# Grouped attention: the weighted sums as plain fp32 products of 64 columns, one product per half of the array

## The chip, the cores and the metric

The kernel runs on one core of one Trainium2 chip. The metric is the device time of one execution in microseconds (us); a kernel's time is the median of several executions. TensorE multiplies matrices into PSUM; VectorE (DVE) and ScalarE (ACT) do the element-wise work, GpSimd (POOL) some filling of memory and some transfers, SyncE (SP) issues most transfers. A product on TensorE has a stationary operand that is loaded first (LDWEIGHTS, the engine row PEld) and a moving operand whose columns are streamed past it (MATMUL, the row PE).

## The reference

A decoder trunk of four layers on 256 tokens of width 2048, in float32. Layer 0 and layer 3 use latent attention, layer 1 sparse grouped attention (each query keeps the 64 keys that an indexer scores highest), layer 2 grouped attention in a window of 128 with a learned sink. Every layer adds four heads of attention to a memory, multiplies all heads by SiLU of a gate, and projects back:

```
for i in range(DEPTH):
    h = _rmsnorm(x, norm_in[i])
    self_out, mq, gate = mixer(h, ...)
    mem_out = _memory_attention(mq, mem_n @ w_mem_kv[i])
    y = concatenate([self_out, mem_out]) * silu(gate)
    x = x + y @ w_out[i]
```

The change touches one line of the two grouped mixers: the weighted sum of the values. There are 32 query heads of width 64 and 4 key/value heads, so that 8 query heads share one value matrix of 64 columns (layer 2 shown; layer 1 sums over the selected keys alone):

```
p = e / (sum(e) + exp(sink - m))
return einsum('bgjqk,bkgd->bqgjd', p, vb)      # j: the 8 heads of group g
```

## The kernel before, in words

All large products are split into parts: an fp32 operand is written as a high part in the format fp32r and a low remainder, also in fp32r, and a product becomes three fp32r products (high by high, high by low, low by high). ACT copies the high part (`copy_act`, L60) and DVE subtracts it to get the low one (L69); `split` does both. The weights `wr` come by DMA in pieces, are split into `wh` and `wl`, and go into `columns_by` (L277, L281) for the projections and into `rows_by` (L257, L258, L259) for the output projection.

Each layer runs over six parts, in the order 4, 0, 1, 2, 3, 5. Parts 4 and 5 are the two pairs of memory heads, parts 0 to 3 the four groups g of 8 heads. A part has a projection of queries (`acc_q`) and of the gate (`acc_g`), attention, and, one part later in the text of the program, its share of the output projection (`w_out`, accumulators `acc_wo`). Each `acc_wo` runs over four slices k of the part's result y: slices 0 and 1 come from the heads 0 to 3 of the group, slices 2 and 3 from the heads 4 to 7.

Within `Grouped.attend` the 8 heads go in the order 0, 2, 1, 3, 4, 6, 5, 7. For each head there are the scores `sp` (L949, L952), the softmax, the normalized weights transposed on TensorE into `ptp` (L516), and a copy of them into SBUF. Heads 0 and 2 share a tile (even), 1 and 3 another (odd), and so on: four heads make what is called a quartet below, and there are 16 quartets in the program (2 layers, 4 groups, 2 each). The weights are split into a high and a low tile of three blocks for each head: queries 0 to 127 by keys 0 to 127, queries 128 to 255 by keys 0 to 127, and queries 128 to 255 by keys 128 to 255. So the products over keys t=0 move 512 columns (2 blocks, 2 heads) and those over t=1 move 256.

The stationary operand is a window of 128 columns of `vz` (L801): the values of the groups, 64 columns each, with 64 columns of zeros between them. Beginning the window at the values or at the zeros before them puts the sum into the upper or the lower half of the 128 output rows and adds zero to the other half. So the even pair and the odd pair of a quartet accumulate into one PSUM tile `o` of 128 rows: rows 0 to 63 even, 64 to 127 odd. Each pair needs six products (two t, three combinations of parts), a quartet twelve (L978). Then DVE multiplies `o` by the gate (`yt`, L984) and splits it into y.

The order of instructions on each engine is not that of the text. A scheduler places them when the program is built, by simulating the engines' timelines; instructions that are marked `keep_in_program_order` keep their order among themselves. Softmax and weighted sums of one group are spread in this way over the projection of the next group and the output projection of the one before. Each engine then runs its own fixed queue in order.

Of the kernel before, what the change touches and what calls it, by code (L numbers as in the profile page):

```python
# [8 lines left out]
F32 = mybir.dt.float32  # L9
# [22 lines left out]
def kernel(ctx: ExitStack, tc: tile.TileContext, a: dict, out: bass.AP,  # L32
# [10 lines left out]
    def misc(name, dt=F32):  # L43
        return ps.tile([P, 512], dt, name=name, tag="mp", bufs=4)
# [8 lines left out]
    def f32(ap):  # L53
        return ap.bitcast(F32)
# [4 lines left out]
    def copy_act(o, i, scale=1.0):  # L59
        inst = nc.scalar.activation(o, i, AF.Copy, scale=scale)  # L60
        if pinned:
            tc.keep_in_program_order(inst)
# [4 lines left out]
    def split(hi, lo, src):  # L67
        copy_act(hi, src)
        nc.vector.tensor_sub(lo, src, f32(hi))  # L69
# [702 lines left out]
    class Grouped:  # L772
# [7 lines left out]
        def first(self):  # L780
            nm, w = self.nm, self.w
            acc = rows_by(nm.at, 16, w, 0, (self.kv0, 512), "kv")
            self.k = act.tile([P, 4, 2, S], F32R, name="kd", tag="big0")
            vs = act.tile([P, 4, S], F32, name="vs", tag="aux", bufs=AUX)
            self.v, self.sel = vs[:, :2, :], vs[:, 2:, :]
            for t in range(2):
                sc = nm.col("rstd", t)
                self.dup(lambda i0, i1: self.k.rearrange("p g v s -> p (g v) s")
                         [:, i0:i1, t * P:(t + 1) * P], acc[t][:, :S], sc, 4)
                copy_act(self.v[:, t, :], acc[t][:, S:], scale=sc)  # L790
            if self.sparse:
                steps.append(self.select())
            else:
                self.spaced_values()

        def spaced_values(self):


            self.vz = [act.tile([P, 2, 9 * 64], F32R, name="vz", tag=f"big{1 + z}") for z in range(2)]
            for z in range(2):  # L800
                nc.gpsimd.memset(f32(self.vz[z]), 0.0)  # L801
            for t in range(2):
                hi, lo = (self.vz[z][:, t, 64:].rearrange("p (g c) -> p g c", c=P)[:, :, :64] for z in range(2))
                split(hi, lo, self.v[:, t, :].rearrange("p (g c) -> p g c", c=64))

        def dup(self, dst, src, sc, n):

# [58 lines left out]
        def selection(self, iqT, ikd, iw, iw2):  # L866

            nc.gpsimd.memset(self.sel[:64, 0, :P], 0.0)
            for b in range(2):
                n = (b + 1) * P  # L870
                rows = slice(0, P) if b else slice(64, P)
                both = spare(0, "sco")
                sco = [both[:, z * S:(z + 1) * S] for z in range(2)]
                cur = 0
                for h in range((8, 16)[b]):
                    sp = misc("isp")
                    rl = wk.tile([P, S], F32, name="rl", tag="e", bufs=4)
                    if b == 0:

                        nc.tensor.matmul(sp[:, :S], iqT[0][:, 2 * h:2 * h + 2, :].rearrange("p h c -> p (h c)"),  # L880
                                         ikd[:, :, :P], start=True, stop=True)
                        lo = wk.tile([P, S], F32, name="isl", tag="z", bufs=3)
                        copy_act(lo[:, :P], sp[:, P:S])
                        nc.vector.tensor_add(lo[:, :P], lo[:, :P], sp[:, :P])
                        nc.scalar.activation(rl[:, :n], lo[:, :P], AF.Relu, scale=0.125)
                        c = iw2[:, h:h + 1]
                    else:
                        for v in range(2):
                            nc.tensor.matmul(sp[:, :S], iqT[1][:, h, :], ikd[:, v, :],
                                             start=v == 0, stop=v == 1)  # L890
                        nc.scalar.activation(rl[:, :n], sp[:, :n], AF.Relu, scale=0.125)
                        c = iw[:, 16 + h:17 + h]
                    if h == 0:
                        nc.vector.tensor_scalar(sco[0][:, :n], rl[:, :n], c, None, op0=OP.mult)
                    else:
                        nc.vector.scalar_tensor_tensor(sco[1 - cur][:, :n], rl[:, :n], c,
                                                       sco[cur][:, :n], op0=OP.mult, op1=OP.add)
                        cur = 1 - cur
                    yield True
                if b == 0:  # L900
                    even = wk.tile([P, S], F32, name="isl", tag="z", bufs=3)
                    nc.scalar.activation(even[64:, :n], sco[cur][:64, :n], AF.Copy)
                    nc.vector.tensor_add(sco[cur][64:, :n], sco[cur][64:, :n], even[64:, :n])
                nc.vector.tensor_add(sco[1 - cur][rows, :n], sco[cur][rows, :n], caus[rows, S - n:])
                cur = 1 - cur
                for it in range(8):
                    m8 = small("m8", 8)
                    nc.vector.max(m8[rows], sco[cur][rows, :n])
                    nc.vector.match_replace(sco[1 - cur][rows, :n], m8[rows], sco[cur][rows, :n], TAKEN)
                    cur = 1 - cur  # L910
                    yield True
                nc.vector.tensor_scalar(self.sel[rows, b, :n], sco[cur][rows, :n], -2e38, NEG,
                                        op0=OP.is_gt, op1=OP.mult)
            self.spaced_values()

        def heads_by_columns(self, dst, acc):

# [22 lines left out]
        def attend(self, g, q, bm, gT):  # L940
            while steps:
                other_work()
            y = act.tile([P, 2, 4, S], F32R, name="y", tag="y", bufs=2)
            for h in (0, 2, 1, 3, 4, 6, 5, 7):
                def score(b):
                    sp = misc("sp")
                    qb = q[h // 4][:, h % 4, b * P:(b + 1) * P]
                    if b == 0:
                        nc.tensor.matmul(sp[:, :S], qb, self.k[:, g, :, :P], start=True, stop=True)  # L949
                    else:  # L950
                        for v in range(2):
                            nc.tensor.matmul(sp[:, :S], qb, self.k[:, g, v, :],  # L952
                                             start=v == 0, stop=v == 1)
                    return sp

                def bias(b, n):
                    bh = bm[:, h, S - n:]
                    if not self.sparse:
                        return bh
                    bs = wk.tile([P, S], F32, name="bs", tag="e", bufs=4)  # L960
                    nc.vector.tensor_add(bs[:, :n], bh, self.sel[:, b, :n])
                    return bs[:, :n]
                nsk = None if self.sparse else nsink[:, g * 8 + h:g * 8 + h + 1]
                tp = masked_softmax(score, bias, None, nsk)

                half, odd = h // 2 % 2, h % 2
                if half == 0:
                    pHL = [wk.tile([P, 3, 2, P], F32R, name="pT2", tag="pT", bufs=PT) for z in range(2)]
                split(pHL[0][:, :, half, :], pHL[1][:, :, half, :],
                      tp[:, :3 * P].rearrange("p (i c) -> p i c", i=3))  # L970
                if half == 0:
                    continue
                if not odd:
                    o = misc("o")
                v0 = g * P + (0 if odd else 64)
                for t in range(2):
                    for n_, (z, p_) in enumerate(((0, 0), (0, 1), (1, 0))):
                        nc.tensor.matmul(o[:, t * S:], self.vz[z][:, t, v0:v0 + P],  # L978
                                         pHL[p_][:, 2 * t:2 + t].rearrange("p i h c -> p (i h c)"),
                                         start=odd == t == n_ == 0, stop=odd == t == 1 and n_ == 2)  # L980
                if odd:
                    j = (h // 4) * 2
                    yt = tmp("yt")
                    nc.vector.tensor_mul(yt.rearrange("p (j b c) -> p j b c", j=2, b=2),  # L984
                                         o.rearrange("p (b j c) -> p j b c", b=2, j=2),
                                         gT[:, j:j + 2, :].rearrange("p j (b c) -> p j b c", b=2))
                    split(y[:, 0, j:j + 2, :], y[:, 1, j:j + 2, :], yt.rearrange("p (a b) -> p a b", a=2))
            return y
# [243 lines left out]
```

## Time and profile before

| what | value |
|---|---|
| time, median of 3 runs | 2577.68 us (2577.62 to 2578.92) |
| span of the profiled execution, first to last instruction | 2576.5 us |
| PE busy, share of the span | 2560.7 us, 99% |
| PEld busy | 2212.3 us, 86% |
| DVE busy | 1928.4 us, 75% |
| ACT busy | 1616.6 us, 63% |
| granted TensorE clock, mean | 0.999 |
| the two grouped layers in the profile | about 980 to 1450 us and 1450 to 1930 us |

The profile shows one execution. Its own time as a run is not listed beside its span; the three runs lie 1.1 to 2.4 us above the span, the median 1.2. In the rows a time is us from the start of the span, and the number behind it the duration. Matmul records overlap at their ends: a record ends when its last results are modelled to be written, while the next has long begun to stream. What a product costs is therefore the distance from one record's end to the next one's, not its duration.

### The profile page before, as it was taken

How to read it: one execution, taken by the hardware profiler on the slowest of the kernel's cores; microseconds unless marked ns; L12 is line 12 of the kernel's file. 1: busy time of each engine (PE TensorE's matmuls, PEld its weight loads, DVE VectorE, ACT ScalarE, POOL GpSimd, SP SyncE). 2: the span in 40 equal slices, each digit the busy share in tenths (PEclk: the TensorE clock that was granted, in tenths of full speed). 3: DMA queues.
4: the chain of work that ended last, by engine and by line, in shares of the span. 5: the costliest groups of instructions: out<-in, count | busy, mean ns of one | idle time of the engine just before them, and what ended most of it. 6: DMA issues, size and time to landing. Idle time of an engine off the chain costs nothing.

```text
span 2576.5 us, 42094 instructions
## 1 busy us (share of the span) xinstructions
PE 2560.7 (99%) x14176; PEld 2212.3 (86%) x14176; DVE 1928.4 (75%) x4234; ACT 1616.6 (63%) x3460; POOL 82.5 (3%) x151
## 2 busy tenths in 40 slices
PE   9999999999999999999999999999999999999998
PEld 7888898888888889888888888888888888888887
DVE  6666667677777787978888777887878767777777
ACT  6556556556656566666666666676666655665665
POOL 1000000000000000000000000000000000000000
PEclk9999999999999999999999999999999999999999
DMA  9888777666677667565656575555554877676654
GB/s 301 256 258 265 241 213 235 186 169 193 196 200 218 203 214 237 169 203 183 204 167 188 168 227 172 172 176 190 185 161 145 241 201 196 195 197 183 210 175 180
DMA packets 477754, 520.04 MB, mean 202 GB/s; under 512 B 69425, under 2 KB 389825, under 8 KB 475873
## 3 DMA queue, kind: packets, MB, share of 16 engines
q1 hardware_dynamic: 460080, 449.71, 57.9%
q0 software_dynamic: 16736, 66.65, 8.1%
q8 instruction: 111, 1.82, 0.3%
q14 instruction: 107, 0.87, 0.1%
q10 hardware_dynamic: 720, 0.98, 0.1%
HBM read 494.10 MB, written 35.75 MB: 206 GB/s over the span
## 4 chain that ended last, share of the span: by engine, by line
PE 97%; DMA 1%; DVE 1%; ACT 0%; issue 0%; SPq 0%; ACTq 0%
PE acc_g L277 14%; PE acc_g L281 7%; PE acc_wo L257 6%; PE acc_wo L258 6%; PE acc_wo L259 6%; PE acc_mq L277 5%; PE acc_mk L277 5%; PE acc_q L277 5%; PE acc_cq L277 3%; PE acc_qn L277 3%; PE acc_mq L281 2%; PE acc_q L281 2%; PE acc_mk L281 2%; PE acc_mv L258 2%; PE acc_mv L257 2%; PE acc_mv L259 2%
## 5 line engine op out<-in xcount | busy, mean ns | idle before, releaser
L69 DVE TENSOR_TENSOR wl<-wr,wh 128x512 fp32r<-128x512 f32 (+1 forms) x1712 | 1160.4, 680 | 568.8 <-ACT wh L60 536.2
L60 ACT ACTIVATE wh<-wr 128x512 fp32r<-128x512 f32 (+1 forms) x1712 | 1064.6, 623 | 813.1 <-PE acc_g L277 175.5
L277 PE MATMUL acc_g<-xT,wh 128*128 128x512 f32 x1536 | 483.9, 396 | 0.0
L281 PEld LDWEIGHTS acc_g<-xT,wl 128*128 128x128 f32 x1536 | 285.2, 188 | 63.9
L281 PE MATMUL acc_g<-xT,wl 128*128 128x256 f32 x1536 | 304.5, 279 | 0.0
L258 PE MATMUL acc_wo<-wl,y 128*128 128x512 f32 x752 | 297.7, 396 | 1.4 <-DVE wl L69 1.3
L259 PE MATMUL acc_wo<-wh,y 128*128 128x512 f32 x752 | 291.8, 390 | 0.0
L257 PE MATMUL acc_wo<-wh,y 128*128 128x512 f32 x752 | 237.3, 394 | 3.1 <-ACT wh L60 2.1
L277 PEld LDWEIGHTS acc_g<-xT,wh 128*128 128x128 f32 x1536 | 234.9, 189 | 0.6
L258 PEld LDWEIGHTS acc_wo<-wl,y 128*128 128x128 f32 x752 | 141.3, 188 | 30.8 <-DVE wl L69 3.6
L257 PEld LDWEIGHTS acc_wo<-wh,y 128*128 128x128 f32 x752 | 138.4, 188 | 34.0 <-ACT y L60 3.8
L259 PEld LDWEIGHTS acc_wo<-wh,y 128*128 128x128 f32 x752 | 141.4, 188 | 26.9
L277 PE MATMUL acc_mq<-xT,wh 128*128 128x512 f32 x512 | 162.3, 397 | 0.0
L277 PE MATMUL acc_mk<-mT,wh 128*128 128x512 f32 x512 | 161.5, 396 | 0.0
L277 PE MATMUL acc_q<-xT,wh 128*128 128x512 f32 x512 | 161.2, 396 | 0.0
L1145 DVE TENSOR_TENSOR x<-x,acc_wo 128x512 f32<-128x512 f32 x184 | 122.2, 683 | 7.6 <-PE acc_wo L259 7.3
L277 PE MATMUL acc_qn<-cT,wh 128*128 128x512 f32 x384 | 121.3, 397 | 0.0
L277 PE MATMUL acc_cq<-xT,wh 128*128 128x512 f32 x384 | 121.0, 396 | 0.0
L281 PEld LDWEIGHTS acc_mk<-mT,wl 128*128 128x128 f32 x512 | 96.1, 188 | 22.8 <-DVE wl L69 0.4
L281 PEld LDWEIGHTS acc_q<-xT,wl 128*128 128x128 f32 x512 | 94.3, 188 | 20.6
L281 PEld LDWEIGHTS acc_mq<-xT,wl 128*128 128x128 f32 x512 | 93.8, 188 | 19.2
L281 PE MATMUL acc_mq<-xT,wl 128*128 128x256 f32 x512 | 104.0, 281 | 0.0
(323 smaller groups left out, 4286.5 us busy)
## 6 DMA issues: line engine op xcount, KB each, us to landing
wr<-in_w_out_dram SPq DMA_DIRECT2D x188, 512.0 KB, 3.7
wr<-in_w_in_a_dram SPq DMA_DIRECT2D x176, 512.0 KB, 4.5
wr<-in_w_mem_kv_dram SPq DMA_DIRECT2D x120, 512.0 KB, 4.6
wr<-in_w_in_b_dram SPq DMA_DIRECT2D x116, 512.0 KB, 3.4
wr<-in_w_in_c_dram SPq DMA_DIRECT2D x104, 512.0 KB, 3.5
wr<-in_w_uq_dram SPq DMA_DIRECT2D x192, 128.0 KB, 2.8
wr<-in_w_uq_dram SPq DMA_DIRECT2D x48, 256.0 KB, 3.8
tab<-flat POOLq DMA_DIRECT2D x8, 1536.0 KB, 9.0
```

Source lines behind the costliest of these rows:

```text
L60: inst = nc.scalar.activation(o, i, AF.Copy, scale=scale)
L69: nc.vector.tensor_sub(lo, src, f32(hi))
L257: nc.tensor.matmul(acc[t][:, :n], xh, wh[:, :n], start=first, stop=False)
L258: nc.tensor.matmul(acc[t][:, :n], xh, wl[:, :n], start=False, stop=False)
L259: nc.tensor.matmul(acc[t][:, :n], xl, wh[:, :n], start=False, stop=last)
L277: nc.tensor.matmul(acc[j], wh[:, o:o + P], q[:, :, kt % 4, :], start=kt == 0, stop=False)
L281: nc.tensor.matmul(acc[j][:, 0, :], wl[:, o:o + P], q[:, 0, kt % 4, :], start=False, stop=kt == kts - 1)
L1145: nc.vector.tensor_add(xs, xs, acc[t])
```

## The change

The spaced copy `vz` is dropped, with its filling by POOL and its splitting. The products take the values themselves, in plain fp32, 64 columns as they lie, and the weights in plain fp32 too. So the low part of the weights and its subtraction on DVE go away: ACT alone copies each head's weights. The even pair's product writes rows 0 to 63 of `o` and the odd pair's rows 64 to 127, each by 64 stationary columns, that is by one half of the columns of the array. A quartet has four products in place of twelve, all issued once the odd pair is ready, in a pinned order: t=0 odd, t=0 even, t=1 odd, t=1 even.

```diff
             if self.sparse:
                 steps.append(self.select())
-            else:
-                self.spaced_values()
-
-        def spaced_values(self):
-            self.vz = [act.tile([P, 2, 9 * 64], F32R, name="vz", tag=f"big{1 + z}") for z in range(2)]
-            for z in range(2):
-                nc.gpsimd.memset(f32(self.vz[z]), 0.0)
-            for t in range(2):
-                hi, lo = (self.vz[z][:, t, 64:].rearrange("p (g c) -> p g c", c=P)[:, :, :64] for z in range(2))
-                split(hi, lo, self.v[:, t, :].rearrange("p (g c) -> p g c", c=64))
...
-            self.spaced_values()
...
             y = act.tile([P, 2, 4, S], F32R, name="y", tag="y", bufs=2)
+            pT = {}
...
                 if half == 0:
-                    pHL = [wk.tile([P, 3, 2, P], F32R, name="pT2", tag="pT", bufs=PT) for z in range(2)]
-                split(pHL[0][:, :, half, :], pHL[1][:, :, half, :],
-                      tp[:, :3 * P].rearrange("p (i c) -> p i c", i=3))
-                if half == 0:
+                    pT[odd] = wk.tile([P, 3, 2, P], F32, name="pT2", tag="pT", bufs=PT)
+                copy_act(pT[odd][:, :, half, :], tp[:, :3 * P].rearrange("p (i c) -> p i c", i=3))
+                if half == 0 or not odd:
                     continue
-                if not odd:
-                    o = misc("o")
-                v0 = g * P + (0 if odd else 64)
+                o = misc("o")
                 for t in range(2):
-                    for n_, (z, p_) in enumerate(((0, 0), (0, 1), (1, 0))):
-                        nc.tensor.matmul(o[:, t * S:], self.vz[z][:, t, v0:v0 + P],
-                                         pHL[p_][:, 2 * t:2 + t].rearrange("p i h c -> p (i h c)"),
-                                         start=odd == t == n_ == 0, stop=odd == t == 1 and n_ == 2)
+                    for e in (1, 0):
+                        tc.keep_in_program_order(nc.tensor.matmul(
+                            o[64 * e:64 * e + 64, t * S:], self.v[:, t, g * 64:g * 64 + 64],
+                            pT[e][:, 2 * t:2 + t].rearrange("p i h c -> p (i h c)"),
+                            start=t == 0, stop=t == 1))
```

The change moves instructions on TensorE. First place: the first products of the first group of layer 1, amid the query projection of the next group. Before, the even pair's first product (L978) stands here, the scores of the next head behind it and its other five products four rows later; the odd pair's six come in the same way some 120 rows below:

```order
L277 MATMUL acc_q_13514<-xT,wh 128x512
L978 MATMUL o<-pT_13062,vz 128x512
L949 MATMUL sp<-kd,qS 128x256
L952 MATMUL sp<-kd,qS 128x256 x2
L281 MATMUL acc_q_13513<-xT,wl 128x256
L281 MATMUL acc_q_13514<-xT,wl 128x256
L277 MATMUL acc_q_13513<-xT,wh 128x512
L277 MATMUL acc_q_13514<-xT,wh 128x512
L281 MATMUL acc_q_13513<-xT,wl 128x256
L281 MATMUL acc_q_13514<-xT,wl 128x256
L978 MATMUL o<-pT_13063,vz 128x512
L978 MATMUL o<-pT_13062,vz 128x512
```

Now (L963, with the scores at L937 and L940), at the end of that projection's first half:

```order
L277 MATMUL acc_q_13477<-xT,wh 128x512
L277 MATMUL acc_q_13478<-xT,wh 128x512
L281 MATMUL acc_q_13477<-xT,wl 128x256
L281 MATMUL acc_q_13478<-xT,wl 128x256
L963 MATMUL o<-pT_13113,vs 64x512
L963 MATMUL o<-pT_13054,vs 64x512
L963 MATMUL o<-pT_13113,vs 64x256
L963 MATMUL o<-pT_13054,vs 64x256
L937 MATMUL sp<-kd,qS 128x256
L940 MATMUL sp<-kd,qS 128x256 x2
L277 MATMUL acc_q_13593<-xT,wh 128x512
L277 MATMUL acc_q_13594<-xT,wh 128x512
```

The four products of a quartet stand together, with products of the full array ahead of them and behind them; so it is for all 16 quartets. Of the 22 rows between the last transposition of the odd pair's weights and the first of the four, the last four are shown.

Second place: the end of the third group of layer 2, where the second quartet's result is wanted by the output projection. The accumulators `acc_wo` with the lower pair of numbers have had slices 0 and 1; their next L257 is slice 2, the first that needs this quartet. Before:

```order
L978 MATMUL o<-pT_20958,vz 128x256
L978 MATMUL o<-pT_20959,vz 128x256
L258 MATMUL acc_wo_22006<-wl,y 128x512
L259 MATMUL acc_wo_22006<-wh,y 128x512
L258 MATMUL acc_wo_22007<-wl,y 128x512
L259 MATMUL acc_wo_22007<-wh,y 128x512
L257 MATMUL acc_wo_21958<-wh,y 128x512
L258 MATMUL acc_wo_21958<-wl,y 128x512
```

Now:

```order
L963 MATMUL o<-pT_20750,vs 64x256
L963 MATMUL o<-pT_20691,vs 64x256
L937 MATMUL sp<-kd,qS 128x256
L940 MATMUL sp<-kd,qS 128x256 x2
L257 MATMUL acc_wo_21766<-wh,y 128x512
L257 MATMUL acc_wo_21767<-wh,y 128x512
L258 MATMUL acc_wo_21766<-wl,y 128x512
L259 MATMUL acc_wo_21766<-wh,y 128x512
L258 MATMUL acc_wo_21767<-wl,y 128x512
L259 MATMUL acc_wo_21767<-wh,y 128x512
L257 MATMUL acc_wo_21718<-wh,y 128x512
```

Between the last product of the quartet and the first row that needs it there were four products of 512 columns; now there are six of 512 and three of 256. In the first three groups of layer 1 the same count goes from six products of 512 columns to ten of 512 and three of 256; in the second group of layer 2 it goes from eight of 512 to six of 512 and three of 256.

## The prediction

> **What bounds the kernel now.** I read the page first: the busy shares and the chain that ended last.
>
> ```profile
> span 2576.5 us, 42094 instructions
> ...
> PE 2560.7 (99%) x14176; PEld 2212.3 (86%) x14176; DVE 1928.4 (75%) x4234; ACT 1616.6 (63%) x3460; POOL 82.5 (3%) x151
> ...
> PE 97%; DMA 1%; DVE 1%; ACT 0%; issue 0%; SPq 0%; ACTq 0%
> ```
>
> 97% of the chain is PE, so what TensorE is spared comes off the time nearly one for one, and what another engine is spared counts only where PE waits for it. The span is 2576.5; the median of the runs, 2577.7, is 1.2 above it, and I add that 1.2 to every span below. Next, the waits of the weight loads within the two grouped layers (980 to 1930 us), because a late operand shows there more fully than in the matmul records, whose modelled ends cover part of it:
>
> ```profile
> PEld acc_wo L257 <- ACT y L60: 3.8, 7, 0.8
> PEld acc_wo L257 <- ACT wh L60: 3.7, 4, 1.2
> PEld acc_wo L258 <- DVE wl L69: 3.6, 6, 1.6
> ```
>
> These 17 waits, 11.1 us by the loads, all lie in the output projection, where a group's attention ends. The timeline of one of them gives the rate at which such a wait becomes lost time:
>
> ```profile
> 1691.70 0.99 PE L978 MATMUL o<-pT,vz 128*128 128x512 f32 x5
> ...
> 1692.84 0.69 DVE L984 TENSOR_TENSOR yt<-o,gT 128x512 f32<-128x512 f32 x1
> ...
> 1693.51 0.40 PE L259 MATMUL acc_wo<-wh,y 128*128 128x512 f32 x1
> 1693.57 0.63 ACT L60 ACTIVATE y<-yt 128x512 fp32r<-128x512 f32 x1
> ...
> 1694.24 0.19 PEld L257 LDWEIGHTS acc_wo<-wh,y 128*128 128x128 f32 x1 [0.78 <-ACT y L60]
> 1694.25 0.50 PE L257 MATMUL acc_wo<-wh,y 128*128 128x512 f32 x1 [0.34 <-ACT y L60]
> ```
>
> L259 ends at 1693.91, the waiting L257 at 1694.75: 0.84 apart, where back-to-back products of 512 columns are 0.23 apart (next fence: 0.63 for two, 0.40 for one). So 0.61 is lost for a load's wait of 0.78, or 0.17 less; all 17 waits lose 11.1 - 17 x 0.17 = 8.2 us. From the last of the products (1692.69) to the first product that needs them there are 1.56 us of DVE and ACT.
>
> **Removed: twelve fp32r products a quartet.** A pair's six are these, one ahead and five together:
>
> ```profile
> 1151.47 0.40 PE L978 MATMUL o<-pT,vz 128*128 128x512 f32 x1
> 1151.71 0.28 PE L949 MATMUL sp<-kd,qS 128*128 128x256 f32 x1
> ...
> 1153.00 0.99 PE L978 MATMUL o<-pT,vz 128*128 128x512 f32 x5
> 1153.83 0.63 PE L277 MATMUL acc_q<-xT,wh 128*128 128x512 f32 x2
> ```
>
> 0.24 and 0.83 (the row of five names the first one's shape: two of 512 columns at 0.23, so 0.12 for each of the three of 256), that is 1.07 a pair, 2.14 a quartet, 34.2 us for the 16.
>
> **Added: four plain fp32 products.** The trace has plain fp32 in latent attention (L527), 32 products in the program:
>
> ```profile
> L527 PE MATMUL o<-pf,vf 128*128 128x128 f32 x64 | 12.2, 272 | 0.0
> ...
> 595.23 0.39 PE L259 MATMUL acc_wo<-wh,y 128*128 128x512 f32 x1
> 595.46 0.38 PE L527 MATMUL o<-pf,vf 128*128 128x128 f32 x2
> ```
>
> There are 64 records for 32 products: an fp32 product is two of them, one after the other. L259 ends at 595.62, the second record at 595.84, so a record of 128 columns takes 0.11. I scale by columns: 0.44 a record at 512, 0.22 at 256. That is a product of 0.88 or 0.44, four times the fp32r one, since the columns pass four times. In sequence a quartet is 2 x 0.88 + 2 x 0.44 = 2.64, half a microsecond more than before. So all hangs on whether the two halves of the array work at once, which no row shows: apart from the one below, all products of the trace use the array's full width. The ends lie between full sequence (2.64) and full overlap (half of it, 1.32). I take the order of issue as binding: a record starts no earlier than the one ahead of it, and one in the same half only when that has streamed. Then the odd product's second record runs beside the even one's first, and the even one's second beside both odd records of t=1: 0.44 alone, 0.44 together, 0.44 together, and the last two of 0.22 alone, 1.76 in all. That the halves do overlap is a judgement: they share neither columns, nor output rows, nor moving data.
>
> **Added: leaving the full array and coming back.** The one product in the trace with another shape of array is the bias table's, 32 by 32:
>
> ```profile
> 69.45 0.61 PE L257 MATMUL acc_mv<-wh,mT 128*128 128x512 f32 x2
> 70.00 0.83 PE L136 MATMUL pt<-oh,rb 32*32 32x384 f32 x2
> 70.75 0.50 PE L258 MATMUL acc_mv<-wl,mT 128*128 128x512 f32 x1
> ...
> L136 PEld LDWEIGHTS pt<-oh,rb x4: 101/103/105, 70.0 to 78.8; 32*32 32x32 f32 x4
> ...
> L978 PEld LDWEIGHTS o<-pT,vz x192: 186/188/193, 1151.2 to 1921.4; 128*128 128x128 f32 x192
> ```
>
> From the end of L257 (70.06) to that of L136 there are 0.77; its two records of 384 columns should take 0.66, so entering cost 0.11. From there (70.83) to the end of L258 (71.25) there are 0.42 in place of 0.23, so leaving cost 0.19. Together 0.30, and a load of 64 columns lies by the two load rows some 0.03 above one of 32: 0.33. The bounds are 0 (a half array might be no such change) and 0.33 (plus a few hundredths); I take 0.33, the only row. The page TensorEngine Tiling (Array Packing) of the Trainium skill, section Key Properties, says that a change of tiling mode drains TensorE, while a change of tile does not; by that rule, with which the 0.30 here agrees, each run of four pays once. The order shows 16 unbroken runs with full-width products on both sides.
>
> Sum for TensorE: 1.76 + 0.33 - 2.14 = -0.05 a quartet, **-0.8 us** for 16.
>
> **Removed on DVE, POOL and ACT.**
>
> ```profile
> L69 DVE TENSOR_TENSOR pT<-ptp,pT 128x384 fp32r<-128x384 f32 x64 | 35.4, 554 | 2.8 <-ACT pT L60 2.6
> L60 ACT ACTIVATE pT<-ptp 128x384 fp32r<-128x384 f32 x64 | 31.3, 489 | 24.3 <-PE ptp L516 23.7
> ...
> L801 POOL MEMSET vz<- x4: 1060/1062/1064, 1039.4 to 1442.7; 128x1152 f32 x4
> ```
>
> DVE loses 64 subtractions, 35.4 us; ACT keeps its 64 copies, at 0.49 each in whatever format. POOL's four fills and the values' split stand off the chain: nothing, since POOL is busy 3% of the time. The 35.4 us are worth only what PE waits for, 8.2 us at most. The y waits (3.8 - 7 x 0.17 = 2.6) should go: between the last product and the row that needs it stood four to eight products of 512 columns (0.9 to 1.8 us) against the 1.56 needed; now stand six to ten and three of 256 (1.7 to 2.7 at 0.23 and 0.12). Of the wl waits (3.6 - 6 x 0.17 = 2.6) I take off half, as DVE has one long instruction less per head there. The wh waits (3.0) come from ACT, which gets nothing: kept. New waits in new places: 0.9. Net **-3.0 us**, bounds -8.2 and, were as many waits added as the y kind had, +2.6.
>
> **The first product waits for the last copy.** Odd goes first, so a run waits once, for the odd copy, and what is queued behind it on PE waits too.
>
> ```profile
> 1688.61 0.38 PE L516 MATMUL ptp<-ident,u 128*128 128x128 f32 x2
> ...
> 1689.34 0.48 ACT L60 ACTIVATE pT<-ptp 128x384 fp32r<-128x384 f32 x1
> ```
>
> From the end of the transposition (1688.99) to the copy's end (1689.82) are 0.83 us; the 22 rows between them in the order, at 0.23 and 0.12, cover over 3. So it costs nothing; without that cover 0.8 each, 13 us.
>
> **The sum**: 2577.7 - 0.8 - 3.0 = 2573.9, said as **2574.0 us**, a span of 2572.8.
>
> **Rivals.**
>
> *The halves take turns* (slower). Then a quartet costs 2.64 + 0.33 - 2.14 = +0.83, 16 make +13.3, and with the 3.0 the time is 2588. For it: no row has two products streaming at once, and the weights' reloading is the only thing that TensorE does beside a stream. Against it: nothing but the argument of separate columns. It decides as soon as less than some 0.3 us of a quartet's 2.64 overlaps. 0.28.
>
> *The halves run side by side in full*: 1.32 + 0.33 - 2.14 = -0.49, 16 make -7.8; 2567. It needs an even record to start with the odd one ahead of its turn; the two records of one product, one behind the other in the row, speak against it. 0.10. The page TensorE: Matmul & The Clock Gate of the Trainium skill, section Part 3: Packing small matmuls, has matmuls on different tiles start about 4 ns apart and a whole pack last hardly longer than one; that is this rival's case, and no trace here shows it.
>
> *The change of shape is free for half an array*: -0.38 a quartet, -6.1; 2568.6. For it: 32 by 32 differs in rows too. 0.10.
>
> *A new wait for y* (slower): a run ends later than six scattered products did, and if the gate product and its copy then queue behind DVE's other work, the output projection waits some 0.5 us at each of 16 quartets, +8, while nothing is relieved: 2585. For it: DVE is 75% busy; against it: the longer cover in the order. 0.06. That the runs are not kept together, with 64 changes of shape, is excluded by the order.
>
> **Numbers.** My forecast has 0.46; its own range is 2569 to 2579, by the bounds of the waits. Over all cases 8 in 10 lie from 2567, the fullest overlap, to 2589, the serial case with a microsecond on it. About 0.2% (5.2 us) is what a measurement can tell from no change. Faster than 2572.5: a third of the forecast (0.15), free change of shape (0.09), full overlap (0.10): 0.34. Slower than 2582.9: 0.27 and 0.05, 0.32. Same: 0.34.
>
> **What would show it.** In the profile after, L963 should have 128 records. A quartet's run, from the end of the product ahead of it to the end of the one behind less that one's 0.23 or 0.12, should last about 2.1: 3.0 would say that the halves take turns, 1.65 that they overlap in full, 1.76 that the change is free. The first record of the even product should end with the odd one's second. The y waits of L257 should be gone and DVE's busy time some 35 us lower. I am wrong if the runs last 2.1 and the time still moves by more than 5 us, or if DVE's relief shows up in no wait at all.

## The result, and the profile after

The changed kernel takes 2560.56 us, median of 4 runs (2560.23 to 2561.52), against 2577.81 us of the kernel before beside it (2577.62 to 2578.92): 17.25 us less, a ratio of 0.9934 with a 95% interval of 0.9922 to 0.9946. The prediction said 2574.0, with a range from 2567 to 2589; the time lies below that range. The profiled execution has a span of 2558.5 us and took 2560.23 us.

The page of the changed kernel, its span, the busy shares and the chain that ended last:

```profile
span 2558.5 us, 41876 instructions
...
PE 2547.5 (100%) x14112; PEld 2190.2 (86%) x14112; DVE 1898.2 (74%) x4166; ACT 1616.4 (63%) x3456; POOL 77.8 (3%) x147
...
PE 99%; DMA 0%; ACT 0%; SPq 0%; DVE 0%; issue 0%; ACTq 0%
```

PE's share of the chain rises from 97% to 99%: it has nearly no one left to wait for. DVE's busy time falls by 30.2 us (1928.4 to 1898.2) where the prediction named some 35, ACT's stays.

The products first. The timeline of the first quartet, with the weight loads, and then the same stretch cut to records that start within a tenth of a microsecond:

```profile
1162.75 0.40 PE L281 MATMUL acc_q<-xT,wl 128*128 128x256 f32 x2
...
1163.07 0.20 PEld L963 LDWEIGHTS o<-pT,vs 128*64 128x64 f32 x4
1163.07 1.51 PE L963 MATMUL o<-pT,vs 128*64 128x512 f32 x8
...
1164.51 0.39 PE L937 MATMUL sp<-kd,qS 128*128 128x256 f32 x1
```

```profile
1163.07 0.65 PE L963 MATMUL o<-pT,vs 128*64 128x512 f32 x2
```

Two records of 512 columns run together from 1163.07 to 1163.72. That is the length of a single one, the longest of the line by the view of the tile:

```profile
L963 PE MATMUL o<-pT,vs x128: 379/486/643, 1163.1 to 1901.8; 128*64 128x512 f32 x64, 128*64 128x256 f32 x64
```

There are 128 records for 64 products, as there should be. The four loads within 0.20 us are those of both halves, for both records of each product. From the end of the product ahead (1163.15) to the end of the score behind (1164.90), less that score's own 0.12, a quartet costs 1.63 us, where twelve products cost 2.14. That is 0.51 less, 8.2 us for the 16 quartets; measured the same way, the other 15 cost the same within 0.02.

Then the waits of the weight loads in the two grouped layers (us in total, number, longest), the view in which the kernel before had three rows with 11.1 us in the output projection. This is the only row of the output projection that is left:

```profile
PEld acc_wo L257 <- ACT wh L60: 0.9, 3, 0.3
```

The rows for y and for wl are gone from it; in the query projection three waits of L281 for wl, 0.6 us together, are new. The largest rows of the view are now 12.1 us before the loads of the four products and 5.4 us before that of the score behind them, which lie within the 1.63 us of the quartets. By the rate of the prediction (0.17 us of each wait is not lost) the loss falls from 8.2 to 0.4 us, a gain of 7.8. Products and waits together make 16.0 of the 17.25 us. The rate comes from a single wait. Added up instead from the ends of all records of the output projection in the two layers, by how much each comes later than is usual for its shape, the loss is 9.0 us before and 0.4 after; with 8.6 for the waits 16.8 of the 17.25 us are accounted for.

### The profile page after: what moved, and what is told of

The parts are those of the page before. It is cut to its first block, busy times and chain, and to the rows that moved or that the text cites. A ratio compares the mean times of both kernels' runs of the same rounds, so it can differ in the third digit from the quotient of the medians.

```text
span 2558.5 us, 41876 instructions
## 1 busy us (share of the span) xinstructions
PE 2547.5 (100%) x14112; PEld 2190.2 (86%) x14112; DVE 1898.2 (74%) x4166; ACT 1616.4 (63%) x3456; POOL 77.8 (3%) x147
## 4 chain that ended last, share of the span: by engine, by line
PE 99%; DMA 0%; ACT 0%; SPq 0%; DVE 0%; issue 0%; ACTq 0%
PE acc_g L277 14%; PE acc_g L281 7%; PE acc_wo L257 7%; PE acc_wo L258 7%; PE acc_wo L259 7%; PE acc_mq L277 5%; PE acc_mk L277 5%; PE acc_q L277 5%; PE acc_cq L277 4%; PE acc_qn L277 3%; PE acc_mq L281 2%; PE acc_q L281 2%; PE acc_mk L281 2%; PE acc_mv L258 2%; PE acc_mv L257 2%; PE acc_mv L259 2%
## 5 line engine op out<-in xcount | busy, mean ns | idle before, releaser
L281 PEld LDWEIGHTS acc_g<-xT,wl 128*128 128x128 f32 x1536 | 285.4, 188 | 64.4
L281 PE MATMUL acc_g<-xT,wl 128*128 128x256 f32 x1536 | 304.6, 280 | 0.0
L257 PE MATMUL acc_wo<-wh,y 128*128 128x512 f32 x752 | 235.7, 392 | 0.0
L257 PEld LDWEIGHTS acc_wo<-wh,y 128*128 128x128 f32 x752 | 138.9, 188 | 28.1 <-ACT wh L60 0.9
L281 PEld LDWEIGHTS acc_mk<-mT,wl 128*128 128x128 f32 x512 | 96.1, 188 | 22.8 <-DVE wl L69 0.4
L281 PEld LDWEIGHTS acc_q<-xT,wl 128*128 128x128 f32 x512 | 93.8, 188 | 20.8 <-DVE wl L69 0.6
L281 PEld LDWEIGHTS acc_mq<-xT,wl 128*128 128x128 f32 x512 | 93.8, 188 | 19.4
L281 PE MATMUL acc_mq<-xT,wl 128*128 128x256 f32 x512 | 104.1, 281 | 0.0
```

What stands on the lines that cost most here:

```text
L257: nc.tensor.matmul(acc[t][:, :n], xh, wh[:, :n], start=first, stop=False)
L281: nc.tensor.matmul(acc[j][:, 0, :], wl[:, o:o + P], q[:, 0, kt % 4, :], start=False, stop=kt == kts - 1)
```

## The experiments

Two questions follow: do the two halves really work side by side, and under which conditions; and why did the waits go, since the prediction took DVE's relief to be the reason and expected 3.0 us of it. In what follows theory D says that DVE's lost subtractions did away with the waits, theory O that the place and the bundling of the products in TensorE's queue did. The kernel before, run beside each group, took 2577.88 and 2577.71 us.

**DVE's subtractions put back.**

```diff
                 if half == 0:
+                    low = wk.tile([P, 3, 2, P], F32, name="pL2", tag="pT", bufs=PT)
                     pT[odd] = wk.tile(...)
                 copy_act(pT[odd][:, :, half, :], ...)
+                nc.vector.tensor_sub(low[:, :, half, :], tp[...], pT[odd][:, :, half, :])
```

> The changed kernel with the 64 subtractions on DVE put back (0.55 us each, 35 us); their result goes into tiles that nothing reads, from the same four buffers as before the change, and TensorE's products stay the four. Theory D (the waits of the output projection went because DVE lost the subtractions): the waits of some 8 us return, 2568.5 us. Theory O (they went because the products now stand together, once the odd pair is ready, and at another place of TensorE's queue): 2560.5 to 2562, with no y or wl waits of the weight loads above 1 us.

Measured: 2561.16 us (2560.83 to 2561.33), ratio 0.9936 (0.9921 to 0.9950): 0.6 us slower than the change. Its busy shares, the row of the subtractions, and the waits of the output projection:

```profile
PE 2549.4 (100%) x14112; PEld 2191.7 (86%) x14112; DVE 1923.6 (75%) x4230; ACT 1615.0 (63%) x3456; POOL 78.2 (3%) x147
...
L959 DVE TENSOR_TENSOR pL<-ptp,pT 128x384 f32<-128x384 f32 x64 | 35.4, 552 | 1.8 <-ACT pT L60 1.4
...
PEld acc_wo L257 <- ACT wh L60: 1.4, 5, 0.3
...
PEld acc_wo L257 <- ACT y L60: 0.8, 3, 0.3
```

The subtractions have their 35.4 us again. DVE's busy time grows by 25.4, because it counts only once a stretch in which two records overlap; it is nearly that of before the change (1923.6 against 1928.4). The waits stay small, 2.2 us against 11.1. DVE's relief is worth 0.6 us, and theory D falls for this kernel. The low parts take buffers out of the same set as before, so the buffers that the change leaves free are not the reason either.

**The kernel before, its twelve products issued once the odd pair is ready.**

```diff
-                if half == 0:
+                if half == 0 or not odd:
                     continue
...
                 for t in range(2):
-                    for n_, (z, p_) in enumerate(((0, 0), (0, 1), (1, 0))):
-                        nc.tensor.matmul(o[:, t * S:], self.vz[z][:, t, v0:v0 + P], pHL[p_][...], ...)
+                    for e in (1, 0):
+                        for n_, (z, p_) in enumerate(((0, 0), (0, 1), (1, 0))):
+                            tc.keep_in_program_order(nc.tensor.matmul(
+                                o[:, t * S:], self.vz[z][:, t, v0:v0 + P], held[e][p_][...], ...))
```

> The kernel before, with the split, the spaced values and all twelve fp32r products of a quartet, but the twelve issued in one pinned sequence once the odd pair is ready, odd first. Theory O: the waits of the output projection go, 2569.5 us. Theory D: DVE still has its subtractions, the waits stay, 2577 to 2579.

Measured: 2572.43 us (2571.74 to 2573.80), ratio 0.9980 (0.9971 to 0.9989): 5.4 us faster than the kernel before with every product and subtraction still there. In the built order one of the twelve stands ahead of other rows and eleven stand together behind them; the sixteen quartets cost 33.9 us in all, as good as the 34.2 of the prediction, so the gain is not in the products. The waits left in the output projection:

```profile
PEld acc_wo L257 <- ACT wh L60: 3.6, 3, 1.2
PEld acc_wo L257 <- ACT y L60: 1.7, 5, 0.5
```

11.1 us have become 5.3, and by the ends of the records the loss falls from 9.0 to 3.8 us, nearly the whole gain. The wl waits are gone and the y waits less than half (3.8 to 1.7), but the wh waits stay as they were (3.7 to 3.6). So the order alone, on the old work, gives more than half of what theory O promised; neither of the two numbers expected was met.

**Four plain fp32 products on the full array.** The values come out of one fp32 copy `vz`, spaced by zeros as before the change.

```diff
-                            o[64 * e:64 * e + 64, t * S:], self.v[:, t, g * 64:g * 64 + 64],
+                            o[:, t * S:], self.vz[:, t, g * P + (0 if e else 64):g * P + (0 if e else 64) + P],
...
```

> The changed kernel's four plain fp32 products, with 128 stationary columns out of a spaced copy of the values (one fp32 copy, filled by POOL, copied by ACT), so on the full array, one after the other, with no change of shape. If the half array's gain is that the two halves run at once, a run lasts 2.6 us in place of 1.64 and the time is 2560.6 + 16 x 1.0 = 2576.5 us with the waits of the output projection still gone; with those waits back 2585. If the halves do not matter (the time came from DVE and the order alone): 2561.

Measured: 2576.21 us (2575.36 to 2577.34), ratio 0.9994 (0.9985 to 1.0003). The first quartet in its timeline, and the only wait of its output projection:

```profile
1163.37 0.40 PE L281 MATMUL acc_q<-xT,wl 128*128 128x256 f32 x2
1163.60 2.74 PE L974 MATMUL o<-pT,vz 128*128 128x512 f32 x8
...
PEld acc_wo L257 <- ACT wh L60: 0.6, 2, 0.3
```

From 1163.77 to 1166.34 are 2.57 us for eight records, one after the other, against 1.63 for the change, the way into the halves of the array and back included. The whole difference between the two kernels, 15.7 us, is 0.98 a quartet. Without the halves the fp32 products would have cost 0.43 more than the twelve; the waits that went pay for that, and the kernel ends where it began (the interval includes no change at all).

**The same four products, each pair's issued as soon as it is ready.** The edit is against the full-array kernel just shown, and it drops the pinned order as well.

```diff
-                if half == 0 or not odd:
+                if half == 0:
                     continue
-                o = misc("o")
+                if not odd:
+                    o = misc("o")
+                v0 = g * P + (0 if odd else 64)
                 for t in range(2):
-                    for e in (1, 0):
-                        tc.keep_in_program_order(nc.tensor.matmul(...))
+                    nc.tensor.matmul(o[:, t * S:], self.vz[:, t, v0:v0 + P], pT[odd][...], ...)
```

> The full-array plain fp32 kernel (four products of 128 columns, spaced values, no subtraction on DVE; 2576.2 us with all four issued after the odd pair) with each pair's two products issued as soon as that pair is ready, as the kernel before did. Same work on every engine; only the order differs. Theory O (the place and bundling of the products did away with the output projection's waits): these come back, up to 9 us, 2580 to 2585. Theory D (DVE's relief did): 2576 as it was.

Measured: 2583.52 us (2582.25 to 2583.91), ratio 1.0022 (1.0013 to 1.0032): 7.3 us slower than with the four together. The waits of its weight loads and its busy shares:

```profile
PEld acc_wo L257 <- ACT wh L60: 7.2, 6, 1.2
PEld acc_wo L257 <- ACT y L60: 1.3, 6, 0.2
...
PEld acc_wo L258 <- DVE wl L69: 0.4, 1, 0.4
...
PE 2565.8 (99%) x14112; PEld 2206.8 (85%) x14112; DVE 1903.0 (74%) x4166; ACT 1614.0 (63%) x3460; POOL 80.5 (3%) x149
```

DVE is as relieved as in the change (1903.0) and the waits are back: 8.9 us in 13 waits, of which 6.7 are lost by the rate used above. With the first experiment this decides against theory D: the relief without the late order has the waits, and the late order with the subtractions put back has hardly any. It doesn't prove theory O in full, since the twelve products, late as well, keep 5.3 us, nearly all of the wh waits among them.

**Both odd products first, then both even ones.**

```diff
-                for t in range(2):
-                    for e in (1, 0):
+                for e in (1, 0):
+                    for t in range(2):
```

> The changed kernel with the four products in another order: both odd ones (t=0, t=1), then both even ones. If each half of the array works through its own products whatever stands between them in the queue, a run stays at 1.64 us and the time at 2560.6. If a record can start no earlier than the one ahead of it in the queue, the even half begins only when the last odd record begins: 0.44, 0.44, 0.22, then 0.22 shared, 0.22 of the even ones' first product left, 0.44, 0.22, 0.22, that is 2.4 us with 0.33 for the change of shape 2.75, and 2560.6 + 16 x 1.1 = 2578 us.

Measured: 2560.09 us (2559.74 to 2560.87), ratio 0.9931 (0.9915 to 0.9948). The first quartet, then the stretch from 1163.57 to 1163.60 alone:

```profile
1163.26 0.40 PE L281 MATMUL acc_q<-xT,wl 128*128 128x256 f32 x2
1163.58 1.52 PE L963 MATMUL o<-pT,vs 128*64 128x512 f32 x8
1165.03 0.39 PE L937 MATMUL sp<-kd,qS 128*128 128x256 f32 x1
```

```profile
1163.58 0.66 PE L963 MATMUL o<-pT,vs 128*64 128x512 f32 x2
```

1.64 us from 1163.66 on, as with the products in turn. The names don't tell the halves apart, but the second of these two records must be the even half's: where one half works alone, a single record starts (the next experiment). So the even half's first record starts together with the odd half's, though two whole odd products stand ahead of it in the pinned order. In both orders each half works through its own products.

**Each pair alone in its half.** The changed kernel with the edit of the early issue above, on half the array and again without pins.

> The changed kernel with each pair's two products issued as soon as that pair is ready, so that a run has products of one half alone: no overlap, 32 changes of shape. A pair costs 0.88 + 0.44 + 0.33 = 1.65, a quartet 3.3 in place of 1.64: 2560.5 + 16 x 1.66 = 2587 us, and with the output projection's waits back up to 2596. If a half-width product were cheaper by itself (without a partner in the other half), about 2561 to 2570.

Measured: 2591.11 us (2590.38 to 2591.83), two runs, ratio 1.0052 (1.0034 to 1.0070). One pair, two products, four records; then the stretch from 1150.6 to 1150.7 alone, and the wait left in the output projection:

```profile
1150.34 0.39 PE L257 MATMUL acc_wo<-wh,y 128*128 128x512 f32 x1
1150.66 1.50 PE L963 MATMUL o<-pT,vs 128*64 128x512 f32 x4
1152.10 0.39 PE L937 MATMUL sp<-kd,qS 128*128 128x256 f32 x1
...
1150.66 0.64 PE L963 MATMUL o<-pT,vs 128*64 128x512 f32 x1
...
PEld acc_wo L257 <- ACT y L60: 4.9, 4, 1.2
```

Four records take as long as eight did: 1.64 us a pair. A record of 512 columns lasts 0.64 us, as long as one that has a partner. Nor does a product get cheaper for having half the columns: the full array took 1.29 us for a pair with the early issue, and 1.64 is that and the 0.33 for the change of shape, which now comes twice as often. The time is within the 2587 to 2596 expected, with a wait for y of 4.9 us back.

**Even first.**

```diff
-                    for e in (1, 0):
+                    for e in (0, 1):
```

> The changed kernel with the even product ahead of the odd one at each t, pinned. The even weights are ready one softmax earlier, so the built order has the first even product alone, some 17 rows ahead of the other three. That is two changes of shape a quartet and one product of 0.88 us without a partner; the remaining three last 1.32 by the longer half (0.88 of the odd t=0, then 0.44) : 0.88 + 0.33 + 1.32 + 0.33 = 2.86 in place of 1.64, 16 x 1.2 = 19.5, 2580 us. If only the number of products counted, 2560.5.

Measured: 2579.83 us (2578.54 to 2580.34), ratio 1.0007 (0.9997 to 1.0017). The first quartet's two pieces:

```profile
1159.44 0.49 PE L516 MATMUL ptp<-ident,e 128*128 128x128 f32 x3
1159.86 1.07 PE L963 MATMUL o<-pT,vs 128*64 128x512 f32 x2
1160.87 0.39 PE L937 MATMUL sp<-kd,qS 128*128 128x256 f32 x1
...
1163.66 0.40 PE L277 MATMUL acc_q<-xT,wh 128*128 128x512 f32 x1
1163.98 1.50 PE L963 MATMUL o<-pT,vs 128*64 128x512 f32 x6
1165.42 0.50 PE L277 MATMUL acc_q<-xT,wh 128*128 128x512 f32 x1
```

1.21 us for the lone product (1159.93 to 1161.26 less 0.12) and 1.63 for the other three, 2.84 in all against 1.63. All of the change's gain is lost by which of two products is written first: the pinned sequence stays in order, but the scheduler puts its first member where that one's operands are ready and other products between it and the rest.

**Eight products in one run.**

```diff
-                if half == 0 or not odd:
+                if h < 7:
                     continue
...
+                for u in (1, 0):
+                    o = misc("o")
                     for t in range(2):
                         for e in (1, 0):
                             tc.keep_in_program_order(nc.tensor.matmul(..., pT[u, e]..., ))
```

> The changed kernel with the eight products of a whole group (two quartets) in one pinned sequence after the group's last head, the second quartet first: 8 runs of eight in place of 16 of four. If a change of shape costs 0.33 us there and back, wherever it stands, 8 of them are saved: 2560.5 - 2.6 = 2557.9 us. If holding the first quartet's tiles to the end of the group makes the output projection wait for y again, as before the change, 2561 to 2566.

Measured: 2557.22 us (2556.33 to 2558.91), ratio 0.9921 (0.9908 to 0.9933): 20.5 us faster than the kernel before and 3.3 faster than the change, the fastest kernel of the study; its slowest run, 2558.91, is below the change's fastest. The first group's run:

```profile
1193.05 0.40 PE L281 MATMUL acc_g<-xT,wl 128*128 128x256 f32 x2
1193.37 2.80 PE L964 MATMUL o<-pT,vs 128*64 128x512 f32 x16
1196.10 0.73 PE L277 MATMUL acc_g<-xT,wh 128*128 128x512 f32 x2
```

2.92 us (1193.45 to 1196.83, less 0.46 for the two products behind) for two quartets that cost 3.26 apart: 0.34 is saved, one change of shape there and back, 2.7 us over 8 groups. (The profile is of the slowest run.) Its grouped layers have no wait of the output projection in the view at all.

## Why the prediction was wrong, point by point

*TensorE bounds the kernel*: right. The gain of products and waits shows in the time nearly one for one (16.8 of 17.25).

*Twelve products cost 2.14 a quartet*: right; issued late, all of them together take 33.9 us. The full-array experiment costs 2.57 a quartet in its run, 0.43 more, and with its waits 1.6 us less than the kernel before in all; the sum (0.43 x 16 less the 7.8 of the waits, -0.9) closes within a microsecond.

*Plain fp32: two records a product, 0.44 and 0.22 each*: right. 128 records; 2.57 us for what was put at 2.64.

*"I take the order of issue as binding"*: **wrong, the first step that failed.** A quartet's products were put at 1.76 and cost 1.30 (1.63 less the 0.33 for the change of shape). That was the rival with 0.10, and its condition, that an even record start ahead of its turn, holds: each half has its own sequence, also when all of the other half's products are queued ahead. The rule of the Trainium skill that stood by that rival, from the page TensorE: Matmul & The Clock Gate, section Part 3: Packing small matmuls, agrees in this: the two records of 0.643 us make a stretch of 0.65 together. What I weighed against it, two records of one product in a row, concerns one half alone. The even product's first record ends with the odd one's first, not with its second. The price of the failure is 7 us.

*Leaving the full array costs 0.33*: right. The run of eight saves 0.34 by one excursion less, and the lone even product costs 1.21 where 0.88 and 0.33 were added. So the rival of a free change (0.10) was wrong. One reading beside it was wrong too: the 32 by 32 product is not the only one that leaves columns idle. The trace before has 32 products of 80 columns (L300, L303), and they follow one another and the full ones at the usual 0.23 and 0.12; no price shows there.

*"Net -3.0 us" for the waits*: **wrong in size and in its reason.** The waits fell by 7.8, near the bound of 8.2. The y waits went, as said; no run tests the longer cover alone. But the wl waits went without DVE's relief (back to 1923.6 us of DVE, 0.6 us slower), which comes close to the prediction's own sign of being wrong, and the wh waits, which I kept because ACT gets nothing, shrank to 0.9 us too. When the fp32 products are issued early on the full array, the wh waits are the largest row again (7.2 us); early in the halves, it is the y waits (4.9). With the twelve products the late order takes away the wl waits and half of the y waits, but not the wh waits (3.6 us). So the order of the queues moves all three kinds, and for wh it needs something else of the change beside it. I had looked at the order only for y, and at the load of the engines for the other two.

*The two errors together*: with the products' 8.2 and the 3.0 of the waits the time would be 2566.5; with the 0.8 of the products and 7.8 of the waits 2569.1. Both lie near the edge of the range; both errors in the same direction give 2561.7, against 2560.6 measured.

*The first product waits for the last copy, hidden*: right, it costs nothing. But there is more to odd first than the prediction saw: it keeps the run in one piece, which is worth 19 us here.

*The serial rival* (0.28) was wrong, and *a new wait for y* did not come. The run lasted 1.63 where I wrote that 2.1 was expected and 1.65 would mean full overlap, so that the test that I named did tell the cases apart.

What stays open: why the scheduler's order with late products leaves fewer waits. That it does is shown by two pairs of kernels with the same products in both orders (5.4 us with twelve, 7.3 with four), but bundling, lateness and the pins were not taken apart. What else takes away the wh waits, which the twelve products keep in the late order too, is open as well: DVE's subtractions and the tile buffers are excluded by the first experiment, and the halves of the array by the full-array one, whose wh waits are 0.6 us. No experiment fixed all other instructions while moving the products alone; each build is scheduled anew.

## What to carry to other kernels

Where two products need only half of the array's columns each, put them in different halves and let them stand together: here a pair cost what one costs, and one alone saved nothing. Count the excursions, that is the ways from the full array to the halves and back, at a third of a microsecond each in these runs, and bundle until that no longer matters. Put the member whose operand is ready last first, so that the bundle isn't taken apart; and when work is moved in a scheduled queue, compare the waits in both orders before crediting them to the engine that was relieved.

## What the runs showed of the hardware that was not expected

The two halves of the array took their products independently of the order between them: the even half's first record started with the odd half's even when four records of the other half were queued ahead of it, and the quartet cost 1.64 us in either order. Plain fp32, with its two records a product, overlaps in full: eight records, four in each half, took 1.51 us, and four in one half alone 1.50. So a product of half the columns was not cheaper by itself: two of them in one half, with the change of shape, took 1.64 us, as did four in both.
